# A feed-forward layer by seven block products, with the second's right sides kept in DRAM

## The chip, the core and the metric

The kernel runs on one core of one Trainium2 chip. The metric is the device time of one execution in microseconds (us). Three runs of the kernel before took 1964.12, 1957.71 and 1943.81 us, median 1957.71.

## What is computed

One layer of a hybrid decoder over x of 1024 positions by 1024 features in float32, D_FF = 2816. The change touches only the last lines:

```
x = x + merged @ w_out[l]
h = rms_norm(x, norm2_g[l])
z = h @ w_ffn_in[l]
x = x + (jax.nn.silu(z[..., :D_FF]) * z[..., D_FF:]) @ w_ffn_out[l]
...
return rms_norm(x, final_g)
```

Ahead of them stand a state-space branch, dilated attention and a convolution branch, whose outputs are merged; the change leaves these as they are.

## The kernel before

Everything lies transposed: 128 features on the partitions, positions along the columns. Activations are eight tiles of 128 x 1024, handled in two halves of 512 columns. Each float32 matmul is made of three on a faster format: a number is split into a high part (a copy rounded to that format) and a low part (the number less the high part), and TensorE sums high x high, high x low and low x high. One weight tile holds up to four 128 x 128 blocks (256 KB): `weights` loads it on SyncE's queue, ScalarE copies the high part (L95), GpSimd subtracts for the low part (L96); two buffers for the load, three each for the parts. `gemms` then issues three matmuls for each block and half (L125 to L127).

`out_proj` adds the product with w_out to x and keeps x1 on the chip (tiles xa); `norm2` scales it (L861, on VectorE, with the factor in PSUM) and splits it into fh and fl (L862 ScalarE, L863 VectorE and GpSimd in turn). `ffn` goes over the 22 units of 128 of D_FF in three groups of 7, 7 and 8 (FFG). `act(j)` makes the two products of a unit, 96 matmuls, and from them silu(a) x b: a tanh on ScalarE (L894), two VectorE operations that read PSUM (L895, L896), and the split into gh (L897) and gl (L898). After each group the second product of that group is added to x1 for all eight m (L938). In the last group the second half of m = 4 to 7 is made in two quarters of 256 columns from weights kept split (`weights_kept`), and `final_norm` (L940) of the first half and of a quarter runs beside matmuls; that of the last quarter ends the kernel. `rstd` (from L130) makes the norm's factor: small matmuls with ones (L139), some small VectorE operations and one ScalarE root, and small matmuls that spread the factor (L154).

Each engine works through its instructions in the order of its own list, which a scheduler makes from the program; a tile's next use waits for its last reader.

## Time and profile before

| | |
|---|---|
| median of three runs | 1957.71 us |
| the profiled execution | 1964.32 us, span 1962.2 us |
| instructions | 23791 |
| busy: PE, VectorE, ScalarE, GpSimd | 96%, 47%, 28%, 31% of the span |
| DMA | 128.97 MB, mean 66 GB/s |
| most of the chain that ended last | PE 72%, of it the three matmul lines L125 to L127 65% |

PE is TensorE's matmul side, PEld its weight loads, DVE VectorE, ACT ScalarE, POOL GpSimd, SP SyncE. A row of the trace gives an operation's line, engine, output and inputs, its size and how long it took. Matmuls are pipelined: one that takes 0.39 us may start 0.23 us after the one before.

### The profile page before, as it was taken

The page shows a single profiled execution, that of the slowest core. Times are in us where ns is not written, and L with a number is a line of the kernel's source. Part 1 is how long each engine was busy: PE and PEld are TensorE (multiplying, and loading weights), DVE is VectorE, ACT ScalarE, POOL GpSimd, SP SyncE. Part 2 cuts the span into 40 slices and gives each one's busy share as a digit, 9 for nine tenths or more (in the row PEclk, how much of TensorE's full clock was granted, in tenths as well). Part 3 has the DMA queues.
Part 4 walks back from the last instruction along what each step waited for, and adds up shares of the span by engine and source line. Part 5 has one row for each costly group of instructions (what it writes and reads, how often), then busy time and mean ns, then how long its engine had stood idle before and what let it go on. Part 6 is the DMA issues. An engine that isn't in the chain of part 4 may idle for free.

```text
span 1962.2 us, 23791 instructions
## 1 busy us (share of the span) xinstructions
PE 1884.1 (96%) x8956; PEld 1492.1 (76%) x8956; DVE 924.3 (47%) x1913; ACT 541.4 (28%) x1023; POOL 601.5 (31%) x519
## 2 busy tenths in 40 slices
...
PEclk9899999897999999899899999999999999999999
...
GB/s 158 97 124 33 39 54 33 70 22 22 28 108 86 54 49 79 57 58 58 81 49 48 49 140 123 87 54 48 48 51 49 49 45 47 54 48 49 49 97 134
DMA packets 94898, 128.97 MB, mean 66 GB/s; under 512 B 14264, under 2 KB 44088, under 8 KB 94784
## 3 DMA queue, kind: packets, MB, share of 16 engines
...
q8 instruction: 71, 1.16, 0.2%
...
## 4 chain that ended last, share of the span: by engine, by line
PE 72%; DVE 7%; POOL 1%; DMA 1%; ACT 1%; issue 1%; SPq 0%; DVEq 0%; ACTq 0%; POOLq 0%
PE ps L126 22%; PE ps L127 22%; PE ps L125 21%; PE ps L388 1%; PE ps L339 1%; DVE zw L644 1%; DVE es L763 1%; POOL wlo L96 1%; PE ps L403 1%; PE ps L768 1%; DVE z L751 1%; PE ps L391 1%; DMA t<-in_xt 1%; PE ps L369 0%; POOL fl L863 0%
## 5 line engine op out<-in xcount | busy, mean ns | idle before, releaser
L96 POOL TENSOR_TENSOR wlo<-wraw,whi 128x512 fp32r<-128x512 f32 x336 | 453.9, 1352 | 1065.8 <-ACT whi L95 1055.0
L95 ACT ACTIVATE whi<-wraw 128x512 fp32r<-128x512 f32 x334 | 208.5, 625 | 828.8 <-PE ps L126 629.5
L125 PE MATMUL ps<-hh,whi 128*128 128x512 f32 x832 | 334.5, 402 | 11.1 <-ACT whi L95 6.3
L126 PE MATMUL ps<-hl,whi 128*128 128x512 f32 x832 | 335.1, 403 | 5.3 <-DVE hl L251 5.3
L127 PE MATMUL ps<-hh,wlo 128*128 128x512 f32 x832 | 332.7, 400 | 0.0
L126 PE MATMUL ps<-fl,whi 128*128 128x512 f32 x704 | 274.1, 389 | 0.5 <-POOL fl L863 0.5
L127 PE MATMUL ps<-fh,wlo 128*128 128x512 f32 x704 | 274.1, 389 | 0.1
L125 PE MATMUL ps<-fh,whi 128*128 128x512 f32 x704 | 274.0, 389 | 0.0
L125 PEld LDWEIGHTS ps<-hh,whi 128*128 128x128 f32 x832 | 159.7, 192 | 50.4 <-issue 9.6
L126 PEld LDWEIGHTS ps<-hl,whi 128*128 128x128 f32 x832 | 159.7, 192 | 42.1 <-DVE hl L251 7.3
L127 PEld LDWEIGHTS ps<-hh,wlo 128*128 128x128 f32 x832 | 159.7, 192 | 37.3 <-issue 5.8
L479 DVE SCALAR_TENSOR_TENSOR cy<-cx,hcw,cy 128x1024 f32<-128x1024 f32 x120 | 165.8, 1382 | 1.0
L126 PEld LDWEIGHTS ps<-fl,whi 128*128 128x128 f32 x704 | 132.2, 188 | 28.3 <-POOL fl L863 0.9
L127 PEld LDWEIGHTS ps<-fh,wlo 128*128 128x128 f32 x704 | 132.2, 188 | 28.3 <-POOL wlo L96 0.9
L125 PEld LDWEIGHTS ps<-fh,whi 128*128 128x128 f32 x704 | 132.2, 188 | 27.3
L125 PE MATMUL ps<-gh,whi 128*128 128x512 f32 x320 | 124.6, 389 | 0.0
L126 PE MATMUL ps<-gl,whi 128*128 128x512 f32 x320 | 124.6, 389 | 0.0
L127 PE MATMUL ps<-gh,wlo 128*128 128x512 f32 x320 | 124.5, 389 | 0.0
L895 DVE SCALAR_TENSOR_TENSOR t<-t,ps 128x512 f32<-128x512 f32 x44 | 30.2, 687 | 187.6 <-ACT t L894 187.6
L938 DVE SCALAR_TENSOR_TENSOR xa<-ps,xa 128x512 f32<-128x512 f32 (+1 forms) x52 | 33.8, 650 | 165.0 <-PE ps L127 165.0
L125 PE MATMUL ps<-ah,whi 128*128 128x512 f32 x256 | 102.1, 399 | 2.6 <-ACT ah L820 2.6
L126 PE MATMUL ps<-al,whi 128*128 128x512 f32 x256 | 102.0, 398 | 1.1 <-DVE al L821 1.1
...
## 6 DMA issues: line engine op xcount, KB each, us to landing
wraw<-in_win SPq DMA_DIRECT2D x120, 256.0 KB, 2.8
wraw<-in_wffi SPq DMA_DIRECT2D x96, 256.0 KB, 2.8
wraw<-in_wffo SPq DMA_DIRECT2D x40, 256.0 KB, 2.6
wraw<-in_wout SPq DMA_DIRECT2D x32, 256.0 KB, 2.8
wraw<-in_wglu SPq DMA_DIRECT2D x16, 256.0 KB, 2.6
t<-in_xt SPq DMA_DIRECT2D x16, 256.0 KB, 3.2
x<-in_xt SPq DMA_DIRECT2D x7, 512.0 KB, 6.8
...
```

The costliest lines, as they stand in the source:

```text
L95: eng.tensor_copy(h, r) if eng else self.A.activation(h, r, AF.Copy)
L96: self.G.tensor_tensor(out=l, in0=r, in1=h.bitcast(F32), op=ALU.subtract)
L125: self.PE.matmul(o, hi[:, k, :], xh[k0 + k][:, t], start=first, stop=False)
L126: self.PE.matmul(o, hi[:, k, :], xl[k0 + k][:, t], start=False, stop=False)
L127: self.mm = self.PE.matmul(o, lo[:, k, :], xh[k0 + k][:, t], start=False, stop=last).ins
L339: self.PE.transpose(ps[:, a, k, :], pt[:, a, k * P:(k + 1) * P], self.ident)
L388: PE.matmul(s[:, 0:256], q1[r, r4, par].rearrange("p b i -> p (b i)"), kp[r, 2 * r4:2 * r4 + 2, :], start=True, stop=True)
L391: PE.matmul(s[c, 256:320], q2[r, r4, par, b], kp[r, j, b::2], start=True, stop=True)
L403: PE.matmul(pv[64 * a:64 * a + 64, (j % 4) * P:(j % 4 + 1) * P], vp[:, 2 * r4 + k, 64 * a:64 * a + 64], ptt[:, a, k, :], start=k == 0, sto ...
L479: V.scalar_tensor_tensor(out=cy, in0=cx[:, j:j + T], scalar=self.hcw[:, ct * TAPS + j:ct * TAPS + j + 1], in1=cy, op0=ALU.mult, op1=ALU.add)
L895: V.scalar_tensor_tensor(out=w, in0=w, scalar=1.0, in1=a, op0=ALU.add, op1=ALU.mult)
L938: self.V.scalar_tensor_tensor(out=x, in0=ps, scalar=0.5, in1=x, op0=ALU.mult, op1=ALU.add)
```

## The change

Both products of the feed-forward layer are made by Strassen's scheme in Winograd's form: the weights are seen as 2 x 2 blocks b11, b12, b21, b22, the right side as well, and seven products of sums of blocks take the place of eight products. The products run in the order 1, 5, 2, 6, 4, 3, 7 and add up in four banks of PSUM (u, y, v, z), which are read between products. For the first product a unit's block rows are its two weight rows j and 22 + j, the block columns of the right side are the two halves of the positions, and the inner blocks are features 0 to 511 and 512 to 1023. A unit now has seven split left sides of 128 x 512 where it had four, three of which are plain weights and four sums (`total`, on VectorE, tile wsum).

The right sides: `norm2(1)` turns x1 in place into the sums and splits them into f1 to f7 (`put`), so x1 is written to DRAM before (xd) and read back later. For the second product `sides(p)` makes seven right sides from units p and p + 11 (tiles ct), each a high and a low part (g1 to g7, 512 KB), writes them to DRAM (ad) and `load_sides` reads them back for groups of pairs (0, 1, 2), (3, 4, 5), (6, 7, 8), (9, 10); pairs 0 and 2 stay on the chip. 17 + 20 slots of 512 KB (l, r) hold all of this; during the first product two of the l slots are free for the seven sides of a pair. `ffn_out` makes two m at a time, 63 matmuls over three pairs or 42 over two; parts of its results go through ScalarE and GpSimd (`aside`). The first products 1 and 2 of three units run before the second half's norm is there (AHEAD). m = 4 to 7 of the last group are made in the old way, in pieces of 512, 256 and 256 columns (`tail`). Weights have six load buffers and four for each part; the pools of the branches are closed before out_proj and new ones opened. `rstd` has two small operations less. The diff's core:

```diff
-FFG = (7, 7, 8)
+NPR = NFF // 2
+GROUPS = ((0, 1, 2), (3, 4, 5), (6, 7, 8), (9, 10))
+AHEAD = 3
...
+KEPT = (0, 2)
+PRODUCTS = (1, 5, 2, 6, 4, 3, 7)
+BANK = {1: "u", 6: "u", 7: "u", 5: "y", 3: "y", 2: "v", 4: "z"}
...
+        def total(p, a, b, op):
+            left[p] = self.wtile("wsum", n)
+            V.tensor_tensor(out=left[p], in0=a, in1=b, op=op)
+            return left[p]
+        for p in sums:
+            if p in (1, 2, 4):
+                left[p] = load({1: 11, 2: 12, 4: 22}[p])
+            elif p == 5:
+                total(5, load(21), load(22), ALU.add)
+            elif p == 6:
+                total(6, left[5], load(11), ALU.subtract)
+                total(7, load(11), load(21), ALU.subtract)
+            elif p == 3:
+                total(3, load(12), left[6], ALU.subtract)
+            hi, lo = self.wtile("whi", n, F32R), self.wtile("wlo", n, F32R)
+            self.split(left[p], hi, lo, self.G)
+            b = BANK[p]
+            first = b not in banks
+            if first:
+                banks[b] = self.psum()
+            o = banks[b]
+            for k, (xh, xl) in enumerate(xc[p]):
+                PE.matmul(o, hi[:, k, :], xh, start=first and k == 0, stop=False, skip_group_check=not first)
+                PE.matmul(o, hi[:, k, :], xl, start=False, stop=False, skip_group_check=not first)
+            for k, (xh, xl) in enumerate(xc[p]):
+                self.mm = PE.matmul(o, lo[:, k, :], xh, start=False, stop=k == n - 1, skip_group_check=not first).ins
+            after[p](banks)
...
+    def right_sides(self, b11, b12, b21, b22, put):
+        V = self.V
+        put(1, b11)
+        V.tensor_tensor(out=b11, in0=b12, in1=b11, op=ALU.subtract)
+        put(5, b11)
+        put(2, b21)
+        V.tensor_tensor(out=b11, in0=b22, in1=b11, op=ALU.subtract)
+        put(6, b11)
+        V.tensor_tensor(out=b21, in0=b21, in1=b11, op=ALU.subtract)
+        put(4, b21)
+        put(3, b22)
+        V.tensor_tensor(out=b12, in0=b22, in1=b12, op=ALU.subtract)
+        put(7, b12)
...
+            early.close()
+            self.bufs = {"wraw": 6, "wsum": 3, "whi": 4, "wlo": 4, "t2": 6, "ct": 6, "g": 6, "s": 2, "l": 17, "r": 20}
+            self.wp = enter(pool("w2"))
+            self.pp = enter(tc.tile_pool(name="ps2", bufs=1, space=PSUM, reuse_waits="tile"))
+            self.lp2 = enter(pool("left"))
+            self.out_proj()
+            right.close()
+            self.rp2 = enter(pool("right", "right"))
+            self.ffn()
+            self.fill(self.rp2, 32)
...
+        def put(p, src, side, eng):
+            z = self.slot(side, f"f{p}")
+            self.split(src, z[:, 0], z[:, 1], eng)
+            self.h2.setdefault(p, []).append((z[:, 0], z[:, 1]))
+        if h == 0:
+            for k in range(KD):
+                scale(k)
+                put(1 if k < half else 2, x1[k][:, 0], "l", self.G if k % 2 else V)
+            return
+        b = [[x1[k][:, 0], x1[k][:, 1], x1[k + half][:, 0], x1[k + half][:, 1]] for k in range(half)]
+        for k, (b11, b12, b21, b22) in enumerate(b):
+            scale(k)
+            V.tensor_tensor(out=b11, in0=b12, in1=b11, op=ALU.subtract)
+            put(5, b11, "r", self.G)
+            scale(k + half)
+            V.tensor_tensor(out=b11, in0=b22, in1=b11, op=ALU.subtract)
+            put(6, b11, "r", self.G)
+        for b11, b12, b21, b22 in b:
+            V.tensor_tensor(out=b21, in0=b21, in1=b11, op=ALU.subtract)
+            put(4, b21, "r", V)
+        for k, (b11, b12, b21, b22) in enumerate(b):
+            put(3, b22, "r", self.G if k % 2 else V)
+        for k, (b11, b12, b21, b22) in enumerate(b):
+            V.tensor_tensor(out=b12, in0=b22, in1=b12, op=ALU.subtract)
+            put(7, b12, "r", self.G if k % 2 else V)
...
+        def silu(x):
+            w = self.tmp([P, 512])
+            A.activation(w, x, AF.Tanh, scale=0.5)
+            V.scalar_tensor_tensor(out=x, in0=w, scalar=1.0, in1=x, op0=ALU.add, op1=ALU.mult)
+        def add(key, b, then=None):
+            def f(banks):
+                V.tensor_tensor(out=r[key], in0=banks[b], in1=r[key], op=ALU.add)
+                if then:
+                    then(r[key])
+            return f
+        def end(banks):
+            for x, key in (("m", "z"), ("n", "y")):
+                add(key, "u")(banks)
+                o = self.wp.tile([P, 512], F32, tag="ct", name="ct", bufs=self.bufs["ct"])
+                V.scalar_tensor_tensor(out=o, in0=r[key], scalar=0.5, in1=r[x], op0=ALU.mult, op1=ALU.mult)
+                self.act.setdefault(j, []).append(o)
+        after = {1: copy("m", "u"), 5: copy("y", "y"), 2: add("m", "v", silu), 6: copy("n", "u"), 4: copy("z", "z"),
+                 3: add("n", "y", silu), 7: end}
+        return self.wino(blocks, half, self.h2, after, banks, skip, only), r
...
+    def sides(self, p):
+        def put(q, src):
+            z = self.slot("r" if p == KEPT[1] and q > 1 else "l", f"g{q}")
+            self.split(src, z[:, 0], z[:, 1], self.V)
+            if p in KEPT:
+                self.first[p, q] = z
+            else:
+                self.nc.sync.dma_start(out=self.ad[p, q], in_=z.bitcast(F32))
+        (b11, b12), (b21, b22) = self.act.pop(p), self.act.pop(p + NPR)
+        if p in GROUPS[-1]:
+            put(0, b12)
+        self.right_sides(b11, b12, b21, b22, put)
+    def load_sides(self, group, products):
+        xc = {}
+        for q in products:
+            for p in group:
+                if p in KEPT:
+                    z = self.first[p, q]
+                else:
+                    z = self.slot("l" if p % 4 == 0 or (p % 4 == 3 and q == 1) else "r", f"g{q}")
+                    self.nc.sync.dma_start(out=z.bitcast(F32), in_=self.ad[p, q])
+                xc.setdefault(q, []).append((z[:, 0], z[:, 1]))
+        return xc
...
+        self.act, self.first = {}, {}
+        order = [j for p in (KEPT[0], *(p for p in range(NPR) if p not in KEPT), KEPT[1]) for j in (p, p + NPR)]
+        begun = {}
+        for j in order[:AHEAD]:
+            begun[j] = self.ffn_in(j, only=(1, 2))
+            if j == order[0]:
+                self.norm2(1)
+        for n, j in enumerate(order):
+            banks, kept = begun.get(j, (None, None))
+            self.ffn_in(j, banks, skip=(1, 2) if banks else (), kept=kept)
+            if n % 2:
+                self.sides(j - NPR)
+        self.x1 = [self.slot("l", "xa", F32) for _ in range(KD)]
+        self.ss = self.slot("l", "ss", F32)
+        for group in GROUPS:
+            last = group is GROUPS[-1]
+            xc = self.load_sides(group, PRODUCTS)
+            n, p0 = len(group), group[0]
+            for m in range(0, KD - KEEP if last else KD, 2):
+                if p0 == 0:
+                    for mm in (m, m + 1):
+                        self.nc.sync.dma_start(out=self.x1[mm], in_=self.xd[mm])
+                self.ffn_out(m, p0, n, xc)
+                if last:
+                    for mm in (m, m + 1):
+                        for h in range(2):
+                            self.sumsq(mm, h)
+        self.tail(p0, n, xc, self.load_sides(group, (0,))[0])
...
+        def aside(x, b):
+            c = self.tmp([P, 512])
+            A.activation(c, b, AF.Copy)
+            G.tensor_tensor(out=x, in0=x, in1=c, op=ALU.add)
+        def end(banks):
+            add(x21, banks["u"])
+            aside(x22, banks["u"])
+        after = {1: lambda b: add(x11, b["u"]), 5: lambda b: aside(x22, b["y"]), 2: lambda b: add(x11, b["v"]), 6: lambda b: add(x12, b["u"]),
+                 4: lambda b: add(x21, b["z"]), 3: lambda b: add(x12, b["y"]), 7: end}
+        self.wino(blocks, n, xc, after)
...
+        for h, t in ((0, slice(0, 512)), (1, slice(0, 256)), (1, slice(256, 512))):
+            for m, (hi, lo) in enumerate(kept, KD - KEEP):
+                ps = self.psum()[:, 0:t.stop - t.start]
+                for k, (xh, xl) in enumerate(halves[h]):
+                    self.PE.matmul(ps, hi[:, k, :], xh[:, t], start=k == 0, stop=False)
+                    self.PE.matmul(ps, hi[:, k, :], xl[:, t], start=False, stop=False)
+                    self.mm = self.PE.matmul(ps, lo[:, k, :], xh[:, t], start=False, stop=k == 2 * n - 1).ins
+                x = self.x1[m][:, h, t]
+                V.tensor_tensor(out=x, in0=ps, in1=x, op=ALU.add)
+                self.sumsq(m, h, t)
+                if m == KD - KEEP and (h, t.start) != (0, 0):
+                    self.final_norm(0 if t.start == 0 else 1, slice(0, 512) if t.start == 0 else slice(0, 256), self.mm)
+        self.final_norm(1, slice(256, 512))
```

Three places in VectorE's list. The first is where the second half's right sides are made. Before (t2 is the scaled tile, L861 scales, L863 splits; then the first unit's silu):

```order
L861 SCALAR_TENSOR_TENSOR t2_9896<-xa3_9005,vecs_66,ps_9879 128x512
L863 TENSOR_TENSOR fl2_9021<-t2_9892,fh2_9013 128x512
L861 SCALAR_TENSOR_TENSOR t2_9900<-xa4_9006,vecs_66,ps_9879 128x512
L861 SCALAR_TENSOR_TENSOR t2_9904<-xa5_9007,vecs_66,ps_9879 128x512
L861 SCALAR_TENSOR_TENSOR t2_9908<-xa6_9008,vecs_66,ps_9879 128x512
L863 TENSOR_TENSOR fl4_9023<-t2_9900,fh4_9015 128x512
L861 SCALAR_TENSOR_TENSOR t2_9912<-xa7_9009,vecs_66,ps_9879 128x512
L863 TENSOR_TENSOR fl6_9025<-t2_9908,fh6_9017 128x512
L895 SCALAR_TENSOR_TENSOR t2_9990<-t2_9990,ps_9916 128x512
L896 TENSOR_TENSOR t2_9990<-t2_9990,ps_9953 128x512
L898 TENSOR_TENSOR gl_9776<-t2_9990,gh_9769 128x512
```

After (the end of the same work: f4, f3, f7 are low parts, L965 the last sums of blocks; the scales and the sums of L954 to L960 stand ahead of these rows; m_9914 is a result of the second unit, wsum_10053 the weight sum of the first unit's third product):

```order
L109 TENSOR_TENSOR f4_9852<-xa_9009,f4_9852 128x512
L109 TENSOR_TENSOR f4_9856<-xa_9010,f4_9856 128x512
L109 TENSOR_TENSOR f4_9860<-xa_9011,f4_9860 128x512
L109 TENSOR_TENSOR f4_9864<-xa_9012,f4_9864 128x512
L109 TENSOR_TENSOR f3_9867<-xa_9009,f3_9867 128x512
L109 TENSOR_TENSOR f3_9873<-xa_9011,f3_9873 128x512
L965 TENSOR_TENSOR xa_9007<-xa_9011,xa_9007 128x512
L109 TENSOR_TENSOR f7_9880<-xa_9005,f7_9880 128x512
L965 TENSOR_TENSOR xa_9008<-xa_9012,xa_9008 128x512
L109 TENSOR_TENSOR f7_9888<-xa_9007,f7_9888 128x512
L1003 TENSOR_TENSOR m_9914<-ps_9922,m_9914 128x512
L128 TENSOR_TENSOR wsum_10053<-wraw_10051,wsum_10010 128x512
```

The first unit's next weight sum has moved behind all of the right sides.

The second place is a unit in the middle of the first product. Before, three operations follow each other for each half of a unit: the two of silu and the low part.

```order
L895 SCALAR_TENSOR_TENSOR t2_9990<-t2_9990,ps_9916 128x512
L896 TENSOR_TENSOR t2_9990<-t2_9990,ps_9953 128x512
L898 TENSOR_TENSOR gl_9776<-t2_9990,gh_9769 128x512
L895 SCALAR_TENSOR_TENSOR t2_10070<-t2_10070,ps_9996 128x512
L896 TENSOR_TENSOR t2_10070<-t2_10070,ps_10033 128x512
```

After (one stretch of a unit that follows a pair's end: ct are the unit's results, g the low parts of the right sides, L163 to L168 their sums, wsum the next unit's weight sums, m a result read from PSUM):

```order
L1012 SCALAR_TENSOR_TENSOR ct_10839<-z_10798,m_10709 128x512
L1012 SCALAR_TENSOR_TENSOR ct_10842<-y_10734,n_10779 128x512
L128 TENSOR_TENSOR wsum_11055<-wraw_11051,wraw_11053 128x512
L109 TENSOR_TENSOR g2_10853<-ct_10839,g2_10853 128x512
L163 TENSOR_TENSOR ct_10685<-ct_10842,ct_10685 128x512
L168 TENSOR_TENSOR ct_10688<-ct_10842,ct_10688 128x512
L165 TENSOR_TENSOR ct_10839<-ct_10839,ct_10685 128x512
L109 TENSOR_TENSOR g6_10858<-ct_10685,g6_10858 128x512
L128 TENSOR_TENSOR wsum_11099<-wsum_11055,wraw_11030 128x512
L1003 TENSOR_TENSOR m_10895<-ps_10928,m_10895 128x512
L109 TENSOR_TENSOR g4_10863<-ct_10839,g4_10863 128x512
L128 TENSOR_TENSOR wsum_11101<-wraw_11030,wraw_11051 128x512
```

The work on the sides stands between the weight sums and the reads of PSUM that the next products need.

The third place is the change from the first to the second product (the last pair's sides; ps_13628 is bank u, which product 6 of the second product adds to next):

```order
L1012 SCALAR_TENSOR_TENSOR ct_13567<-z_13526,m_13437 128x512
L1012 SCALAR_TENSOR_TENSOR ct_13570<-y_13462,n_13507 128x512
L128 TENSOR_TENSOR wsum_13768<-wraw_13764,wraw_13766 128x384
L109 TENSOR_TENSOR g2_13579<-ct_13567,g2_13579 128x512
L163 TENSOR_TENSOR ct_13413<-ct_13570,ct_13413 128x512
L168 TENSOR_TENSOR ct_13416<-ct_13570,ct_13416 128x512
L165 TENSOR_TENSOR ct_13567<-ct_13567,ct_13413 128x512
L109 TENSOR_TENSOR g6_13583<-ct_13413,g6_13583 128x512
L109 TENSOR_TENSOR g4_13587<-ct_13567,g4_13587 128x512
L109 TENSOR_TENSOR g3_13590<-ct_13570,g3_13590 128x512
L109 TENSOR_TENSOR g7_13594<-ct_13416,g7_13594 128x512
L1083 TENSOR_TENSOR xa_13597<-ps_13628,xa_13597 128x512
```

The first read of bank u (L1083) stands behind the last pair's low parts g2, g6, g4, g3 and g7; before, there was no such place, since a group's low parts came one at a time.

## Rows read from the trace of the kernel before

**Rows 1.** The page: busy time and share of each engine; granted clock in tenths.

```profile
PE 1884.1 (96%) x8956; PEld 1492.1 (76%) x8956; DVE 924.3 (47%) x1913; ACT 541.4 (28%) x1023; POOL 601.5 (31%) x519
PEclk9899999897999999899899999999999999999999
```

**Rows 2.** Stretches: length, busy time and count of PE, PEld, DVE, ACT, POOL; clock, DMA share, GB/s.

```profile
8.00:12.00 4.00, 3.83 (x12) 2.66 (x13) 2.24 (x4) 2.97 (x4) 2.51 (x2) 1.00 1.03 412
...
1222.00:1262.00 40.00, 37.88 (x175) 30.52 (x174) 20.13 (x30) 20.01 (x31) 23.77 (x17) 1.00 0.29 97
1262.00:1900.00 638.00, 638.00 (x2816) 528.47 (x2815) 125.69 (x169) 134.22 (x222) 165.35 (x132) 1.00 0.17 53
...
1927.10:1951.40 24.30, 24.30 (x205) 24.29 (x204) 14.99 (x36) 7.49 (x16) 0.00 (x0) 1.00 0.22 71
1951.40:1962.20 10.80, 1.85 (x14) 1.52 (x13) 4.62 (x15) 0.62 (x2) 0.00 (x0) 0.70 0.29 97
```

**Rows 3.** Grouped lines from 1222 us on: count, busy us, mean ns, idle before.

```profile
L96 POOL TENSOR_TENSOR wlo<-wraw,whi 128x512 fp32r<-128x512 f32 x135 | 176.2, 1306 | 432.4 <-ACT whi L95 426.9 <-DMA wraw<-in_wffi 2.8 <-PE ps L126 2.7
...
L95 ACT ACTIVATE whi<-wraw 128x512 fp32r<-128x512 f32 x134 | 84.6, 632 | 338.6 <-PE ps L126 239.4 <-issue 79.3 <-DMA wraw<-in_wffi 16.6
...
L898 DVE TENSOR_TENSOR gl<-t,gh 128x512 fp32r<-128x512 f32 x44 | 39.3, 892 | 34.7 <-ACT gh L897 34.7
...
L896 DVE TENSOR_TENSOR t<-t,ps 128x512 f32<-128x512 f32 x44 | 30.2, 687 | 149.1 <-PE ps L127 148.8
...
L894 ACT ACTIVATE t<-ps 128x512 f32<-128x512 f32 x44 | 26.0, 591 | 47.8 <-PE ps L127 45.8 <-POOL fl L863 1.9
...
L96 POOL TENSOR_TENSOR wlo<-wraw,whi 128x384 fp32r<-128x384 f32 x16 | 16.2, 1012 | 64.6 <-ACT whi L95 64.6
...
L947 DVE SCALAR_TENSOR_TENSOR o<-xa,vecs,ps 128x256 f32<-128x256 f32 x16 | 6.4, 475 | 2.1 <-PE ps L154 2.1
...
L861 DVE SCALAR_TENSOR_TENSOR t<-xa,vecs,ps 128x512 f32<-128x512 f32 x8 | 5.6, 739 | 1.3 <-PE ps L154 1.3
...
L938 DVE SCALAR_TENSOR_TENSOR xa<-ps,xa 128x256 f32<-128x256 f32 x8 | 3.4, 422 | 6.1 <-PE ps L127 6.1
```

**Rows 4.** Timeline of DVE and POOL: start, duration (us), engine, line, operation.

```profile
1244.78 1.12 DVE L863 TENSOR_TENSOR fl<-t,fh 128x512 fp32r<-128x512 f32 x1
1245.31 1.75 POOL L96 TENSOR_TENSOR wlo<-wraw,whi 128x512 fp32r<-128x512 f32 x1
...
1263.83 1.30 POOL L96 TENSOR_TENSOR wlo<-wraw,whi 128x512 fp32r<-128x512 f32 x1 [1.79 <-ACT whi L95]
1264.30 1.37 DVE L898 TENSOR_TENSOR gl<-t,gh 128x512 fp32r<-128x512 f32 x1 [2.76 <-ACT gh L897]
...
1283.15 1.30 POOL L96 TENSOR_TENSOR wlo<-wraw,whi 128x512 fp32r<-128x512 f32 x1 [4.15 <-ACT whi L95]
1283.59 0.69 DVE L895 SCALAR_TENSOR_TENSOR t<-t,ps 128x512 f32<-128x512 f32 x1 [2.31 <-ACT t L894]
...
1292.16 0.69 DVE L898 TENSOR_TENSOR gl<-t,gh 128x512 fp32r<-128x512 f32 x1 [0.70 <-ACT gh L897]
```

**Rows 5.** Timeline, second half's norm2: its first scale and its last split.

```profile
1241.54 2.06 DVE L861 SCALAR_TENSOR_TENSOR t<-xa,vecs,ps 128x512 f32<-128x512 f32 x3 [1.31 <-PE ps L154]
...
1249.98 1.73 POOL L863 TENSOR_TENSOR fl<-t,fh 128x512 fp32r<-128x512 f32 x1
```

**Rows 6.** DMA issues: count, KB of one, median us from issue to landing.

```profile
wraw<-in_wffi SPq DMA_DIRECT2D x96, 256.0 KB, 2.8
...
x<-in_xt SPq DMA_DIRECT2D x7, 512.0 KB, 6.8
...
ud<-uw SPq DMA_DIRECT2D x4, 512.0 KB, 3.0
```

**Rows 7.** Timeline, the end: first add after the last matmul, last norm's scales.

```profile
1951.66 0.42 DVE L938 SCALAR_TENSOR_TENSOR xa<-ps,xa 128x256 f32<-128x256 f32 x1 [1.45 <-PE ps L127]
...
1955.71 3.22 DVE L947 SCALAR_TENSOR_TENSOR o<-xa,vecs,ps 128x256 f32<-128x256 f32 x8 [0.87 <-PE ps L154]
```

212 lines of the change are left out of this document (97 added, 115 removed).

## The prediction

> **What bounds the kernel now.** I read the busy times and the clock first: TensorE is busy 96% of the span, at close to the full granted clock [rows 1]. The feed-forward part is then cut into stretches [rows 2]. It begins at 1222.0. From 1262 to 1900 TensorE is never idle: 2816 matmuls in 638.0 us, one every 0.2266 us, at the full 2.4 GHz (granted clock 1.00). VectorE is busy 20% there, ScalarE 21%, GpSimd 26%, and DMA moves 53 GB/s. In the 24.3 us from 1927.1 to 1951.4 it makes 205, of which 192 are over 256 columns and the rest small ones of the norm: 0.12 us each. After the last one, 10.8 us of closing norm and output follow [rows 2, 7]. So this part is bound by the count of matmuls, and each one less gives its 0.2266 us for as long as the other engines hand over operands in time.
>
> **What is removed.** Before, each of 22 units takes 96 matmuls in the first product and 48 in the second: 3072 of 512 columns and 192 of 256. After: 22 x 84 = 1848 in the first; 4 x 63 x 3 + 2 x 42 = 840 in the second's seven-product part; in the tail 48 of 512 and 96 of 256 columns. That is 336 full and 96 half matmuls less: 336 x 0.2266 + 96 x 0.120 = 76.1 + 11.5 = 87.6 us. This is the most the change can give.
>
> **What is added, in the steady state of the first product.** A unit now lasts 84 x 0.2266 = 19.0 us, a pair 38.1. In a pair ScalarE makes 14 weight copies, 12 moves out of PSUM or tanh and 7 side copies, some 20 us by [rows 3] (0.63 and about 0.6 each): half of the time. GpSimd subtracts 14 weights x 1.30 = 18.2 us. VectorE does 8 additions that read PSUM (0.69) and 27 operations whose two inputs both lie in SBUF: 8 weight sums, 8 of the gate, 4 sums and 7 low parts of the right sides.
>
> The second kind has no fixed price. In [rows 4] one took 0.69 us with GpSimd idle. The one at 1264.30 came while GpSimd subtracted (1263.83 to 1265.13) and ended at 1265.67, 0.54 us after it: it had waited. At 1244.78 and 1245.31 it goes the other way too: GpSimd's 1.75 us end 1.16 us after VectorE's end. A PSUM reader inside such a time (1283.59) keeps its 0.69. So the two engines take turns, at about 0.54 and 1.16 us. A pair needs 27 x 0.54 + 14 x 1.16 = 30.8 us of turns out of 38.1: 81%, which fits. VectorE's own time is 27 x 0.89 (the mean with GpSimd at 26%) + 8 x 0.69 = 29.6 us at the low end; with 1.0 each 32.5; at the 1.37 of a full wait 42.5, over the pair's 38.1. I take 1.0: GpSimd is about half busy, and half of the 0.68 lies between 0.69 and 1.37. PE then loses only small waits. I put them at 5 us over the eleven pairs, with 0 and 49 us (11 x 4.4) as ends.
>
> The Trainium skill (GPSIMD Engine Reference, Key points) says that GpSimd shares its SBUF interfaces with VectorE and contends with VectorE instructions that have two SBUF inputs. The trace agrees (0.69 against 1.37 us). That rule speaks against this change; what it could cost is the first rival below.
>
> **The sides' way through DRAM.** Only two slots take each pair's seven 512 KB tiles, so the third must wait for the first's write. By order and durations, with 0 at a unit's last matmul: the third side's low part ends at 4.9, is in DRAM at 7.9 (3.0 us [rows 6]), the fifth's copy can start then, and ScalarE reaches it at 8.8; it waits about 1 us for the sixth and hardly for the seventh. Behind these copies on ScalarE stand weight copies that PE wants 5 to 10 us later (four buffers of 2.7 us). A stall begins where a write takes about 8 us. Rate: 65 writes and their reads are 34 MB each; a pair moves 8 weight tiles and 7 sides, 5.7 MB in 38 us, 150 GB/s, against 412 GB/s in the opening burst [rows 2]. I cost it at nothing, with rival 2 as the other end.
>
> **The second product.** A pair of rows m lasts 63 x 0.2266 = 14.3 us. GpSimd: 7 x 1.01 + 2 x 1.3 to 1.5 = 10 us. VectorE: 6 x 0.69 + 4 x about 0.6 = 6.6. Both fit. At a group's change 21 sides are wanted; seven load ahead, the other 14 (7.3 MB, 18 us at 412 GB/s) while the last 14.3 us of the old group free their slots, in the order of use. The last is wanted 12 us into the new group: no wait. If they started only there, 18 - 12 = 6 us at each of three changes: ends 0 and 18 us, an end of the range and no case of its own.
>
> **Where PE must wait anew.**
> 1. norm2 of the second half. In the kernel before eight scales and eight splits there took from 1241.5 to 1251.7 [rows 5], and PE lost 2.1 us in the stretch [rows 2]. Now the third product's weight sum of the first unit stands on VectorE behind all work on the right sides (first order piece): 8 scales x 0.74, 24 operations with two SBUF inputs, which alternate with GpSimd's 12 splits and 3 weights (24 x 0.54 + 15 x 1.16 = 30 us of turns). Adding the steps gives the sum at about 31 us after the scale factor is there, its high and low part at 33 to 34, and the seventh product's end at 37. PE has 87 matmuls = 19.7 us of work for that time. Wait: 17 us (12 if all run at 0.69 and 1.30; 20 at most). I add 3 us for a lower granted clock after it (it was 0.70 in the closing stretch, where PE was mostly idle), ends 0 and 7, and 3 for the small matmuls of the norm, which exist before too.
> 2. From the first to the second product. TensorE (PE in the rows) has 18 matmuls (4.1 us) and then the second side's 9 (2 us). The add that frees bank u for product 6 stands behind nine operations with two SBUF inputs (third piece): 2 x 0.69 + 11 x 0.7 = 9.3 us without, about 12.5 with waits for GpSimd. Wait: 12.5 - 6.1 = 6 us (3 to 8).
> 3. At out_proj the new pools start on freed memory, so the third weight load waits for the branches' end: one load and split, 2.5 us (0 to 6).
> 4. The tail. PE needs 96 x 0.120 = 11.5 us for the half matmuls, but VectorE has the whole first half's final norm now beside them (8 x 0.74 = 5.9), the next quarter's (8 x 0.475 = 3.8), eight adds and six sums at 0.42 (5.9) and two chains of small ones (2): 17.6 us, then the closing 10.8. With 1 to 2 us of waits that is 30 us, 8 more than PE's count gives.
>
> **The sum.** 1222.0 + 2.5 + 2736 full matmuls x 0.2266 (620.0) + norm2 17 + 3 + 3 + transition 6 + small waits 5 + tail 30 = 1908.5 us of span. Before: 1962.2, with 2.1 us around it (time 1964.3). So 1910.6 against 1964.3: 53.7 us less. The profiled execution is as slow as the slowest of the three runs (1964.1); set against the median of 1957.7 the same gain ends at 1904. I say 1906.
>
> **The rivals.**
> 1. GpSimd and VectorE block each other: VectorE's operations with two SBUF inputs take over 1.21 us in the mean ((38.1 - 5.5) / 27), and VectorE sets the pace. At 1.25 to 1.37, +12 to +49 us: 1918 to 1955. For: single rows at 1.37. Against: 81% of turns, and L898's mean of 0.89 [rows 3]. 18%.
> 2. Slower: the two write-back slots. If a 512 KB write beside weight loads takes more than 8 us, ScalarE stands in its order before the copy of the fifth side and the weights behind it come late. At 11 us the four rounds cost about 6 us in each of nine to ten pairs, +57: 1963 and more. For: a 512 KB load took 6.8 us in the burst. Against: the writes in the trace took 3.0, at a third of the burst's rate. 8%.
> 3. The new waits are mostly hidden (norm2 at 8, transition 2, tail 3 less): about 1888. 12%.
>
> **How the numbers follow.** The forecast has 60% (1893 to 1920); 2% are for what I don't see. Leaving out rival 2 and the dearer half of rival 1 gives the range 1880 to 1945. A measurement can tell about 1% here, that is 20 us. Faster by more (under 1938): forecast, rival 3 and nearly half of rival 1, 80%. Within 1%: most of the rest of rival 1, 11%. Slower: rival 2 and a little of rival 1, 9%.
>
> **What would show it.** 84 matmuls in 19.0 us with no gap in the middle of the first product (right), or PE gaps released by GpSimd's wlo or VectorE's wsum (rival 1). wlo near 1.5 and the side subtractions near 1.0 us. Writes of the sides at 3 us to landing, ScalarE's waits for them under 2 us a pair (else rival 2). A gap of some 17 us, in pieces, at the right sides of norm2, 6 us at the change of product, none at the group changes. VectorE busy to the end of the tail. I am wrong above all if VectorE and GpSimd queue on each other more than one operation deep.

## The result, and the profile after

The changed kernel takes 1904.0 us in the median (runs of 1930.33, 1897.12, 1907.48 and 1900.52). The kernel before, measured beside it, takes 1957.8 us. The ratio is 0.972, with a 95% interval from 0.965 to 0.980. The ratio leaves out the run of 1930.33 us, which was in the slow state. So the change makes the kernel 2.8% faster, and the forecast of 1906 us holds.

The profile shown here is that of the 1930.33 us execution. Between 500 and 600 us its granted clock was 0.81, in work that the change does not touch, so all that follows starts late. Therefore I compare lengths of stages between events and not the times at which they happen. The page first: busy times, the granted clock in tenths, then the issues of the new transfers (count, KB of one, median us from issue to landing).

```profile
PE 1824.1 (95%) x8524; PEld 1430.1 (74%) x8524; DVE 1214.8 (63%) x2271; ACT 668.6 (35%) x1282; POOL 776.9 (40%) x659
...
PEclk9899999897969999999999999979999999999998
...
ad<-g SPq DMA_DIRECT2D x65, 512.0 KB, 2.8
g<-ad SPq DMA_DIRECT2D x65, 512.0 KB, 6.7
```

Against [rows 1], TensorE (PE) has 432 matmuls fewer and is busy 60 us less. VectorE (DVE) is busy 290 us more and GpSimd (POOL) 175 us more. The feed-forward part runs from its first matmul at 1241.2 to the end at 1928.5: 687.3 us, where it took 740.2 before (1222.0 to 1962.2). That is 52.9 us less. It falls into a first product of 445.1 us (to the first matmul that reads a side g), a second of 200.0 (to the first of the tail) and a tail of 42.2.

The stretches of that part, as in [rows 2]: length, busy time and count of PE, PEld, DVE, ACT and POOL, then granted clock, DMA share and GB/s.

```profile
1256.00:1300.00 44.00, 28.52 (x95) 19.60 (x94) 37.79 (x42) 20.41 (x35) 27.26 (x20) 0.77 0.10 33
1300.00:1685.00 385.00, 384.56 (x1697) 318.19 (x1697) 288.16 (x362) 187.90 (x338) 201.11 (x143) 1.00 0.43 154
1685.00:1700.00 15.00, 10.18 (x38) 7.97 (x37) 10.34 (x16) 5.81 (x11) 4.18 (x4) 0.89 0.89 331
...
1886.10:1911.80 25.70, 25.70 (x174) 23.74 (x172) 18.28 (x35) 9.02 (x18) 1.30 (x1) 1.00 0.19 68
1911.80:1928.50 16.70, 4.26 (x23) 3.85 (x21) 9.27 (x30) 0.97 (x4) 0.00 (x0) 0.59 0.43 147
```

In the second row lies nearly the whole first product: 385 us in which PE is idle for 0.44 us, with a matmul every 0.227 us at the full clock, while VectorE is busy 75% of the time. So the saving of the removed matmuls arrives whole in the steady state. What is given back lies at three places: the norm of the second half (first row), the change from the first product to the second (third row), and the tail (the last two). Of the 87.6 us that the removed matmuls are worth, this part gives back 34.7: by the stages about 20 at the norm (22.5 less the 2.1 lost there before), 6 at the change of product and 9 in the tail.

PE's four longest waits from 1200 us on (engine, line, what it waited for: total us, times, longest) name them:

```profile
PE ps L149 <- DVE m L1003: 9.0, 1, 9.0
PE ps L214 <- DVE sm L208: 5.1, 2, 3.2
PE ps L149 <- DMA g<-ad: 4.8, 1, 4.8
PE ps L150 <- POOL f L109: 4.2, 5, 1.5
```

The first and the fourth are the norm, the third is the change of product, the second is the closing norms.

### The profile page after: what moved, and what is told of

Its sections match the earlier page's. It is cut to its first block, busy times and chain, and to the rows that moved or that the text cites. A ratio compares the mean times of both kernels' runs of the same rounds, so it can differ in the third digit from the quotient of the medians.

```text
span 1928.5 us, 24417 instructions
## 1 busy us (share of the span) xinstructions
PE 1824.1 (95%) x8524; PEld 1430.1 (74%) x8524; DVE 1214.8 (63%) x2271; ACT 668.6 (35%) x1282; POOL 776.9 (40%) x659
## 4 chain that ended last, share of the span: by engine, by line
PE 45%; DVE 2%; issue 1%; DMA 1%; POOL 1%; ACT 0%; SPq 0%; DVEq 0%; ACTq 0%; POOLq 0%
PE ps L149 10%; PE ps L150 10%; PE ps L152 10%; PE ps L188 4%; PE ps L187 4%; PE ps L186 4%; DVE f L109 0%; PE ps L1115 0%; PE ps L1116 0%; PE ps L1117 0%; DMA g<-ad 0%; POOL f L109 0%; DVE o L1133 0%; PE ps L200 0%; PE ps L214 0%
## 5 line engine op out<-in xcount | busy, mean ns | idle before, releaser
L103 POOL TENSOR_TENSOR wlo<-wraw,whi 128x512 fp32r<-128x512 f32 x184 | 257.8, 1404 | 574.8 <-ACT whi L102 569.2
L186 PE MATMUL ps<-hh,whi 128*128 128x512 f32 x832 | 334.9, 403 | 11.2 <-ACT whi L102 6.3
L102 ACT ACTIVATE whi<-wraw 128x512 fp32r<-128x512 f32 x182 | 114.0, 629 | 418.7 <-PE ps L187 335.6
L149 PE MATMUL ps<-f,whi 128*128 128x512 f32 x616 | 242.4, 394 | 11.7 <-DVE m L1003 9.0
L150 PE MATMUL ps<-f,whi 128*128 128x512 f32 x616 | 242.3, 393 | 4.2 <-POOL f L109 4.2
L109 POOL TENSOR_TENSOR wlo<-wsum,whi 128x512 fp32r<-128x512 f32 (+2 forms) x144 | 179.3, 1250 | 158.2 <-ACT whi L108 104.3
L186 PEld LDWEIGHTS ps<-hh,whi 128*128 128x128 f32 x832 | 160.0, 192 | 50.7 <-issue 10.3
L109 POOL TENSOR_TENSOR wlo<-wraw,whi 128x512 fp32r<-128x512 f32 (+2 forms) x108 | 142.2, 1317 | 99.4 <-ACT whi L108 66.7
L152 PE MATMUL ps<-f,wlo 128*128 128x512 f32 x616 | 165.8, 391 | 0.0
L149 PEld LDWEIGHTS ps<-f,whi 128*128 128x128 f32 x616 | 116.7, 189 | 38.0 <-ACT f L108 13.0
L150 PEld LDWEIGHTS ps<-f,whi 128*128 128x128 f32 x616 | 116.6, 189 | 31.3 <-POOL f L109 7.5
L152 PEld LDWEIGHTS ps<-f,wlo 128*128 128x128 f32 x616 | 116.2, 189 | 24.1
L149 PE MATMUL ps<-g,whi 128*128 128x512 f32 x280 | 109.9, 393 | 4.9 <-DMA g<-ad 4.8
L108 ACT ACTIVATE whi<-wsum 128x512 fp32r<-128x512 f32 (+2 forms) x144 | 82.9, 578 | 84.0 <-PE ps L150 69.4
L150 PE MATMUL ps<-g,whi 128*128 128x512 f32 x280 | 109.4, 391 | 0.0
```

The lines of the kernel that those rows point to most:

```text
L102: eng.tensor_copy(hi, raw) if eng else self.A.activation(hi, raw, AF.Copy)
L103: self.G.tensor_tensor(out=lo, in0=raw, in1=hi.bitcast(F32), op=ALU.subtract)
L108: self.A.activation(hi, src, AF.Copy)
L109: eng.tensor_tensor(out=lo, in0=src, in1=hi.bitcast(F32), op=ALU.subtract)
L149: PE.matmul(o, hi[:, k, :], xh, start=first and k == 0, stop=False, skip_group_check=not first)
L150: PE.matmul(o, hi[:, k, :], xl, start=False, stop=False, skip_group_check=not first)
```

## Experiments

All of them start from the changed kernel. Where only one profile was taken, a whole time tells little, since the granted clock between 200 and 600 us differs from run to run (0.91 to 1.00) and moves the start of the feed-forward part (1209.7 to 1241.2 us in these profiles). Inside that part the stages repeat where an edit leaves them alone: the first product within about 0.5 us, the tail within 0.7 and the second product within 1.6 (199.4 to 201.0). The verdicts rest on them. Three kernels with four times each come last.

| kernel | time, us | first product | second product | tail |
|---|---|---|---|---|
| the changed kernel, profiled | 1930.33 | 445.1 | 200.0 | 42.2 |
| e1_bank | 1901.09 | 445.3 | 200.1 | 41.9 |
| e2_wsum_pool | 1930.23 | 457.5 | 204.2 | 42.1 |
| e5_hook | 1898.87 | 444.5 | 201.0 | 42.0 |
| e6_f56_vector | 1914.36 | 443.6 | 200.3 | 41.9 |
| e7_write2 | 1903.95 | 445.7 | 201.0 | 41.9 |
| e3_write3 | 1980.65 | 511.8 | 203.7 | 41.8 |
| e8_loads_outproj | 1899.44 | 445.5 | 195.5 | 42.3 |
| e4_tail_halves | 1902.84 | 445.2 | 199.4 | 44.3 |
| e9_ahead4 | 1921.80 | 447.7 | 200.8 | 42.1 |
| e10_three | 1908.68 (median) | 448.7 | 195.8 | 42.3 |
| e11_five | 1905.75 (median) | 441.7 | 196.0 | 42.3 |
| e12_four | 1897.70 (median) | 442.7 | 197.1 | 42.5 |

### Who ends the wait at norm2

The longest wait, 9.0 us, ends with an add that reads a PSUM bank (m, L1003). The prediction had named another operation, the weight sum of product 3. Both stand on VectorE behind the work on the right sides. The first run writes `norm2(1)` one unit later in the program, so that the second unit's add comes ahead of the sides.

```diff
...
             if j == order[0]:
-                self.norm2(1)
+                bc = self.rstd(self.squares.pop(0), D, self.mm)
+            if j == order[1]:
+                self.norm2(1, bc)
```

> In the changed kernel PE waits 9.0 us at product 4 of the first unit, and the trace names the VectorE addition of m (L1003) as what ended it: the second unit's product 2 still holds the PSUM bank that product 4 wants, and its reader stands on VectorE behind all of the right sides' work. Here the norm's factor is made at the same place, but the work on the right sides is written behind the second unit's first two products, so that this one read moves ahead of it; nothing else changes. Theory A (the bank): the 9.0 us split: product 4 starts when its fourth side is split, some 5 us earlier, and PE then waits 4 to 6 us for the third product's weight sum, which is still last; the stretch from the factor to the seventh product's end (about 39 us) is 1 to 3 us shorter. Theory B (the weight sum alone decides, as the prediction had it): the end of the seventh product does not move (within 0.7 us), though product 4 may move. Rival C (the order matters for neither, the turns of VectorE and GpSimd do): no wait changes by more than 1 us.

The wait for m is gone, and another stands 12 matmuls later, at product 3 of the same unit:

```profile
PE ps L149 <- ACT whi L108: 6.0, 1, 6.0
```

This is the high part of product 3's weight sum. The first product takes 445.3 us, as before. So the bank was merely the first of two operations in one queue, and taking it away shortens nothing.

The second run moves all weight sums from VectorE to GpSimd.

```diff
-            V.tensor_tensor(out=left[p], in0=a, in1=b, op=op)
+            self.G.tensor_tensor(out=left[p], in0=a, in1=b, op=op)
```

> All weight sums (4 a unit) are made by GpSimd and no longer by VectorE. If the two engines take turns at 0.54 us (VectorE) and 1.16 us (GpSimd) for operations with two SBUF inputs, a pair's turns grow from 27 x 0.54 + 14 x 1.16 = 30.8 us to 19 x 0.54 + 22 x 1.16 = 35.8 us of the pair's 38.1, 94%, and GpSimd's own time is 22 x 1.3 to 1.4 = 29 to 31 us. Theory A (turns): it still just fits; PE loses 0 to 1.5 us in a pair, 0 to 15 us over the first product (385 us between 1300 and 1685 in the changed kernel), and wlo's mean rises towards 1.4. Theory B (engines independent, only own time counts): no loss at all, VectorE at 50% and wlo at 1.30. Theory C (a chain of three GpSimd steps for a product is too late whatever the shares): over 2 us a pair, over 22 us in all. In the second product GpSimd gets 11 x about 1.0 + 2 x 1.5 = 14 us for 14.3 us of matmuls, so PE waits there too, 0 to 2 us a pair of rows, 14 pairs.

The first product grows by 12.4 us and the second by 4.2. GpSimd's sides come late (PE waits 8.7 us for POOL f, 4.2 before), the wait for m stays at 8.3, and waits for low parts and loads grow. In the middle of the product GpSimd is now busy 335 of 385 us (201 before), and the same operations take longer on both engines (grouped lines of this run between 1283 and 1668 us: count, busy us, mean ns, idle before):

```profile
L109 DVE TENSOR_TENSOR g<-ct,g 128x512 fp32r<-128x512 f32 x73 | 95.5, 1311 | 44.4 <-ACT g L108 44.2
L109 POOL TENSOR_TENSOR wlo<-wsum,whi 128x512 fp32r<-128x512 f32 x81 | 129.4, 1598 | 34.7 <-ACT whi L108 33.9 <-PE ps L152 0.5
```

In the changed kernel these means are 875 and 1375 ns. So the theory of independent engines is refuted, and the loss lies in the range of the theory of turns. Work that goes from one of the two engines to the other does not leave the turns that both take. How much of the 12.4 us is waiting for turns the run does not tell, since GpSimd also needs about 1.3 us for an operation that VectorE makes in 0.69.

The third run writes product 3's weight sum and the adds ahead of the last eight sides (f3 and f7), so that both known waits are served early.

```diff
...
+            if p in hooks:
+                hooks[p]()
...
```

The hook makes f3 and f7, behind the split of product 3's weight sum.

> Only the order around the first unit's third product is changed: the fourth sides are split first, then the weight sum of product 3 and its split, and only then the third and seventh sides; the second and third unit's additions of m, which free PSUM banks, come ahead of these too. The run before this one freed the bank alone, and PE's 9.0 us at product 4 turned into 6.0 us at product 3, with the first product's length unchanged (445.4 against 445.1 us). Theory (the place in VectorE's order decides, as the prediction said, with two things behind the sides' work, a bank and a weight sum): now both are ahead, product 4 starts some 5 us earlier, product 3 follows within 1 to 3 us, and the first product (first to last of its matmuls) takes 437 to 440 us, 5 to 8 us less. Rival (the amount of work on VectorE and GpSimd in turns is what lasts, wherever the sum stands): the seventh sides come last in any order, less than 2 us gained.

Both waits are gone, and the first product is only 0.6 us shorter, hardly more than it repeats within. The whole first product, in the changed kernel and in this run (columns as above):

```profile
1241.20:1686.34 445.14, 429.22 (x1873) 351.54 (x1872) 334.28 (x418) 216.95 (x386) 234.32 (x166) 0.98 0.40 142
```

```profile
1209.69:1654.17 444.48, 433.32 (x1874) 352.34 (x1872) 321.03 (x418) 220.22 (x386) 242.09 (x166) 0.98 0.40 142
```

PE's idle time did fall, from 15.9 to 11.2 us, but its matmuls take 4.1 us more. The stretch from 1226.5 to 1268.5 holds 97 matmuls in 42 us at a granted clock of 0.76, much as the 44 us of the changed kernel hold 95 at 0.77, although it has 9.5 us of idle time and not 15.5. The idle time is in more pieces, and the last matmul before each piece counts with its whole length (0.39 us at the full clock and not 0.227). The rows don't divide these two. VectorE's rows show where the pieces come from (start, duration, engine, line, operation, what it waited for):

```profile
1236.55 0.69 DVE L959 TENSOR_TENSOR xa<-xa 128x512 f32<-128x512 f32 x1 [1.36 <-POOL f L109]
...
1249.41 1.18 DVE L970 TENSOR_TENSOR xa<-xa 128x512 f32<-128x512 f32 x1
1250.51 1.76 DVE L109 TENSOR_TENSOR f<-xa,f 128x512 fp32r<-128x512 f32 x1
```

Operations of one shape take 0.69, 1.18 or 1.76 us, by what GpSimd does beside them. The wait has been cut into pieces that the next operations of the same queue end. The fourth run takes work out of the turns instead: the eight low parts of sides 5 and 6 are made on VectorE, at 0.69 us each, and no longer on GpSimd at 1.3.

```diff
-            put(5, b11, "r", self.G)
+            put(5, b11, "r", V)
...
-            put(6, b11, "r", self.G)
+            put(6, b11, "r", V)
```

> In the second half's norm2 the low parts of the fifth and sixth sides (8 operations) are made by VectorE and no longer by GpSimd. If the engines take turns at 0.54 and 1.16 us, the turns fall from 24 x 0.54 + 15 x 1.16 = 30.4 to 32 x 0.54 + 7 x 1.16 = 25.4 us, while VectorE's own list grows from 24 x 0.69 + 8 x 0.74 = 22.5 to 28 us without waits. Theory A (turns): VectorE waited for GpSimd most of the difference before, so the stretch stays within 2 us of what it was (first product 445 us, 443 to 446), though GpSimd does 8 operations less. Theory B (independent engines, VectorE's own time decides): 5.5 us longer, 450 to 451. Theory C (GpSimd's part was the bound, its low part of each side had to be there before the next sum in place): 4 us or more shorter, under 441.

The first product is 1.5 us shorter, within the range of the theory of turns (443 to 446) and against that of independent engines (450 to 451). Here too PE's idle time falls by more, from 15.9 to 12.0 us, and its matmuls take 2.4 us longer; in the first of the four runs the two are 13.0 and 3.1. Together: no single operation sets the length of the norm. Three edits took 2.9 to 4.8 us of idle time away, slower matmuls took most or all of it back, and the gain is 1.5 us or nothing. That the rest is set by the amount of work in turns fits these rows but is not shown: the third run ends its last side 4.5 us later than the changed kernel (50.7 us after the first matmul, against 46.2) and loses nothing by it.

### The two slots and the writes to DRAM

The prediction's rival on the slow side put a threshold at a write of 8 us. Two runs write each side again into other DRAM tiles, which makes the time longer for which a slot is held, and adds DMA traffic and issues on SP.

```diff
...
                 self.nc.sync.dma_start(out=self.ad[p, q], in_=z.bitcast(F32))
+                self.nc.sync.dma_start(out=self.ad2[p, q], in_=z.bitcast(F32))
+                self.nc.sync.dma_start(out=self.ad3[p, q], in_=z.bitcast(F32))
```

The last line stands in the run with three writes alone. Two writes:

> Each right side is written to DRAM twice. With one write (2.8 us to landing) PE lost nothing in the middle of the first product, with three (a slot held 5.3 to 7.1 us from the first issue to the last landing) it lost 66.8 us, so the point at which the two slots decide lies below 7 us and not at the 8 us of the prediction. Here a slot is held about 4 to 4.5 us. If the loss begins in proportion from about 3 us on: 20 to 30 us lost (first product 465 to 475 us). If there is a point near 5 us, below which the weight loads behind the writes on SyncE's queue still come in time: 0 to 8 us lost (445 to 453).

The first product takes 445.7 us. A write lands in 4.2 us in the median, and a slot is held, from the first issue to the last landing, for 5.0 us in the median (4.0 to 7.4). ScalarE's waits for the writes grow only from 11.8 to 13.3 us in all. Three writes:

> Each split right side is written to DRAM three times (to three places) where the changed kernel writes it once, so a slot comes free only when all three writes have landed; DMA in the first product rises from about 154 to about 350 GB/s. This puts the two write-back slots to the test. Theory A (the slack worked out before: no stall until a write takes about 8 us): the three land 5 to 8 us after the first is issued, ScalarE's waits for them grow from 12 us in all to 40 to 80 us, and PE loses 0 to 10 us in the first product. Rival (slots are the next bound, little slack): PE loses over 2 us a pair, 20 us and more. The weights' loads, from 2.8 us to landing, may rise to 4 to 5 us; they have six buffers.

Now the first product takes 66.7 us more: 53.6 of idle PE and 13.1 of slower matmuls. Most of the idle time is one kind of wait (total us, times, longest), and the chain that ends the longest one shows how it comes about (start, us, what):

```profile
PE ps L149 <- ACT whi L108: 53.4, 7, 25.2
```

```profile
1634.16 4.43 DMA ad<-g
...
1638.69 0.64 ACT g L108
1639.35 0.70 DVE g L109
1640.07 0.32 SPq L1029
...
1641.43 4.91 DMA ad<-g
...
1650.83 4.93 DMA wraw<-in_wffi
...
1655.85 0.70 DVE wsum L128
...
1656.64 0.64 ACT whi L108
1657.32 0.79 PE ps L149
```

A write frees its slot, ScalarE and VectorE make the next side in it, and SP issues that side's writes. The next weight load stands behind them on SP, and PE waits for its sum. The mechanism of the rival is right, but its threshold was too high: slots held for 5.0 us in the median cost nothing, and slots held for 6.8 us in the median (5.2 to 8.9) cost 66.7 us. The two ranges overlap, and both are wider than the expectations have them (4 to 4.5 and 5.3 to 7.1 us), so no single time is shown to be the limit. The three writes also fill the DMA (0.73 busy against 0.43, and weight loads land in 4.2 us instead of 2.8), so a part of that price may be the loads'. These runs don't divide it.

### The change of product, and out_proj

At the change of product PE waited 4.82 us for a load of a side (DMA g<-ad), and not for the add on VectorE that the prediction had named. The loads of pair 1 were issued together from 1685.40 on, behind a weight load on SP. At out_proj, PE waited for the high part of a weight:

```profile
1143.85 0.39 PE L188 MATMUL ps<-ah,wlo 128*128 128x512 f32 x1
1148.76 0.79 PE L186 MATMUL ps<-mh,whi 128*128 128x512 f32 x1 [4.52 <-ACT whi L102]
1149.35 0.63 PE L187 MATMUL ps<-ml,whi 128*128 128x512 f32 x1
```

That weight copy stands on ScalarE behind a copy of mh that is ready only at 1147.56. One run removes both causes: it loads pair 1's sides ahead of the last pair's sides, and makes the high part of out_proj's first two weights on GpSimd.

```diff
+            if p == KEPT[1] and q == 5:
+                for i in PRODUCTS:
+                    self.first[1, i] = self.slot("r", f"g{i}")
+                    self.nc.sync.dma_start(out=self.first[1, i].bitcast(F32), in_=self.ad[1, i])
...
-                hi, lo = self.ahead.pop(0) if self.ahead else self.weights(src[:, k0:k0 + m, :], m)
+                hi, lo = self.ahead.pop(0) if self.ahead else self.weights(src[:, k0:k0 + m, :], m, self.engs.pop(0) if self.engs else None)
...
+        self.engs = [self.G, self.G]
...
-                if p in KEPT:
+                if (p, q) in self.first:
```

> Two edits in places far apart. First, the seven loads of pair 1's sides for the first group of the second product are put ahead of the last pair's own sides, so that they take slots that come free 13.6 us before the change of product and stand ahead of weight loads on SyncE's queue. In the changed kernel PE waits 4.8 us there for such a load, issued at 1685.4, when PE was already through with the first product. Theory (the loads stood behind a weight load that waited for its buffer): the wait for a load goes, and what remains is the read of bank u behind the last sides on VectorE, 2 to 4 us, as the prediction had it at 6: 1 to 3 us gained. Rival (DMA has no room there, 331 GB/s in that stretch): the loads land as late as before. Second, the first two weights of out_proj get their high part on GpSimd and not on ScalarE. In the changed kernel PE waits 4.5 us there: ScalarE's copy stands behind the last high part of the merged activations. Theory (order on ScalarE): the wait shrinks to under 1 us and the half clock after it goes, 4 to 6 us gained. Rival (the buffers, closed pools): the wait stays above 3 us.

The second product is 4.5 us shorter, more than the theory's 1 to 3. The wait for the loads is gone, and a smaller one is left there, for a side that VectorE makes last:

```profile
PE ps L151 <- DVE g L110: 1.9, 1, 1.9
```

At out_proj the 4.5 us are gone as well, and the way from the first mh matmul to the feed-forward part takes 91.0 us instead of 92.4 (91.1 in the kernel before). Thus out_proj cost 4.5 + 1.4 = 5.9 us, the second part as matmuls at the lower of the two clock levels after the gap (0.43 us apart instead of 0.227). The gain at out_proj holds with the six raw-weight buffers of this run; with five, below, more than half of it is lost.

### The tail

The tail makes its last 512 columns in two pieces of 256. This run makes them whole.

```diff
-        for h, t in ((0, slice(0, 512)), (1, slice(0, 256)), (1, slice(256, 512))):
+        for h, t in ((0, slice(0, 512)), (1, slice(0, 512))):
...
```

> The tail's last 512 columns are made whole instead of in two quarters (48 matmuls of 512 columns for 96 of 256), so one final norm of 512 columns closes the kernel where two of 256 did. In the changed kernel the stretch from 1886.1 to the end takes 42.4 us: 25.7 with PE busy, then 16.7, in which VectorE still has the quarter before last. Theory A (VectorE is the tail's bound, PE's count is not): VectorE saves one chain of small operations and 16 x 0.475 become 8 x 0.74, three adds and sums fall away; the closing stretch shrinks to 12 to 14 us and the PE stretch to 22 to 23, 35 to 37 in all: 5 to 7 us gained. Theory B (the quarters hide half of the last norm, as in the kernel before): 4 to 6 us lost, since a whole norm of 512 columns (5.9 us) stands behind the last matmul instead of 3.2.

The tail grows by 2.1 us: the way of theory B, though less than its 4 to 6, and against theory A. The rows of VectorE show it (start, duration, engine, line, operation):

```profile
1877.52 5.36 DVE L1133 SCALAR_TENSOR_TENSOR o<-xa,vecs,ps 128x512 f32<-128x512 f32 x8 [0.33 <-PE ps L214]
1882.80 1.28 DVE L1119 TENSOR_TENSOR xa<-ps,xa 128x512 f32<-128x512 f32 x2
...
1891.62 5.36 DVE L1133 SCALAR_TENSOR_TENSOR o<-xa,vecs,ps 128x512 f32<-128x512 f32 x8 [2.23 <-PE ps L214]
```

The first half's closing norm, 5.36 us, stands ahead of the last adds in both kernels. In whole columns the second one takes 5.36 us at the very end, where the pieces leave 3.22.

### One more unit ahead, and the edits together

The products 1 and 2 of three units run ahead of the sides. A fourth needs one more buffer for t2, which comes from the raw weights.

```diff
-AHEAD = 3
+AHEAD = 4
...
-            self.bufs = {"wraw": 6, "wsum": 3, "whi": 4, "wlo": 4, "t2": 6, "ct": 6, "g": 6, "s": 2, "l": 17, "r": 20}
+            self.bufs = {"wraw": 5, "wsum": 3, "whi": 4, "wlo": 4, "t2": 7, "ct": 6, "g": 6, "s": 2, "l": 17, "r": 20}
```

> One more unit's products 1 and 2 are multiplied ahead of the norm (AHEAD 4 instead of 3; one raw-weight slot less and one more t2 slot for it): 24 more matmuls of 0.226 us, 5.4 us, move into the time in which VectorE and GpSimd make the seven sides, and 24 fewer stand behind it. Theory A (PE waits there because the work of VectorE and GpSimd between the scale factor and the last sides takes longer than the products that are ahead; nothing else waits): the first product takes 440 (445.1 minus 5.4). Theory B (the unit's 24 weights need sums and splits by the same engines that make the sides, so the cover brings its own work with it): each of its products 1 and 2 needs weight sums on VectorE and low parts on GpSimd, and the first product stays within 1.5 us of 445.

Neither theory is right: the first product takes 447.7, which is 2.6 us more. PE's order tells why nothing is gained. Only product 1 of the fourth unit stands ahead; its product 2 stands behind product 6 of the first unit, and PE waits there for a bank:

```profile
1277.61 0.80 PE L149 MATMUL ps<-f,whi 128*128 128x512 f32 x1 [7.29 <-DVE m L1003]
```

```profile
1286.75 0.77 PE L149 MATMUL ps<-f,whi 128*128 128x512 f32 x1 [9.02 <-DVE m L1003]
```

The first row is of this run, the second of the changed kernel. In both, PE has made 96 matmuls of the first product by then. That took 48.2 us here (from 1229.38) and 45.6 there (from 1241.20). The cover didn't grow: the fourth unit's 12 matmuls took the place of 12 others (product 5 of the first unit), and the bank came 2.7 us later. Whether the unit's own weights or the raw-weight buffer that it cost made the bank late is not shown, as the run changes both.

Three edits together (the fourth unit, the earlier loads, out_proj's weights):

> Three edits together: one more unit ahead of the norm, pair 1's sides loaded ahead of the last sides' writes, and the high part of the first two out_proj weights on GpSimd. Theory A (the three waits are apart and their gains add): transition -4.5, out_proj's wait -4.5 to -5.5, the norm between 0 and -5.4: 1889 to 1895 beside a run of the changed kernel at 1900.5, ratio to before about 0.966. Theory B (taking one wait away only moves it to the next): 1897 or more.

The ratio to the kernel before is 0.973 (0.969 to 0.978), not to be told from the changed kernel's. The expectation was put in whole times, and its case for 1897 or more came true. By stages the first two edits do about what they did alone: 448.7 in the first product (e9: 447.7) and 195.8 in the second (e8: 195.5). At out_proj they do not. PE waits there again, for the high part that GpSimd now makes, and the way from the first mh matmul to the feed-forward part takes 94.7 us (e8: 91.0):

```profile
1134.80 0.80 PE L187 MATMUL ps<-mh,whi 128*128 128x512 f32 x1 [2.68 <-POOL whi L103]
```

With five raw-weight buffers the second weight's load is issued 5.3 us later than in e8, just when the first mh matmul starts. So the buffer that the fourth unit took brings back more than half of what the edit at out_proj gained. From the end of the matmuls before out_proj to the end of the kernel the three edits save 2.8 us, which the whole times can't show.

Five edits (those three, the weight sum ahead of f3 and f7, and sides 5 and 6 on VectorE):

> The three edits of the run before, and the two that gave 0.6 and 1.5 us in the first product (product 3's weight sum written ahead of the last sides; the low parts of products 5's and 6's sides on VectorE). Theory A (all add): 1887 to 1893, 2 us under the three. Theory B (the order at the norm is used up, as the amount of work in turns sets its end): within 1.5 us of the three edits' time.

The ratio is 0.973 (0.968 to 0.979), and the median 2.9 us below that of the three. By stages the first product falls by 7.0 us against the three edits, to 441.7, which is more than the 2.1 that the two added edits gave alone. Neither theory had that. Out_proj still takes 94.8 us.

Four edits (the five without the fourth unit):

> The five edits without the fourth unit ahead of the norm. With it the run of one edit lost 2.6 us in the first product (447.7 against 445.1) and the run of five gained 3.4 (441.7). Theory A (the fourth unit ahead holds two more PSUM banks until the sides are done, so that it only moves the wait, and it loses the same 2.6 us among the five): without it the first product takes 439. Theory B (once product 3's weight sum and the sides' low parts are out of the turns, the banks come free in time and the fourth unit's 24 matmuls do cover something): without it the first product takes 443.0, that is 445.1 minus the 0.6 and 1.5 that the two edits gave alone. Second product 195.5 and tail 42.3 by both.

The first product takes 442.7, as the theory of added gains has it (445.1 - 0.6 - 1.5 = 443.0). So in the first product the fourth unit costs 2.6 us alone and gains 1.0 beside the other four edits. The ratio is 0.971 (0.964 to 0.978). By stages this version's feed-forward part takes 682.3 us and that with five edits 679.9, against 687.3. But with six raw-weight buffers out_proj takes 91.0 us again, against 94.8 with five, and from the first mh matmul to the end the four edits need 773.3 us and the five 774.7: with the buffer that it costs, the fourth unit gains nothing. The whole times can't tell these from the changed kernel: the start of the feed-forward part spreads over more than they gain.

## Why the prediction was right

**The steady state.** The prediction took VectorE's operations with two SBUF inputs at 1.0 us in the mean, GpSimd's subtractions near 1.5, and small waits of 5 us. The grouped lines between 1300 and 1685 us (count, busy us, mean ns, idle before):

```profile
L109 DVE TENSOR_TENSOR g<-ct,g 128x512 fp32r<-128x512 f32 x74 | 64.4, 875 | 22.4 <-ACT g L108 22.0
L128 DVE TENSOR_TENSOR wsum<-wsum,wraw 128x512 f32<-128x512 f32 x20 | 29.9, 1495 | 21.5 <-POOL wlo L109 21.5
L1012 DVE SCALAR_TENSOR_TENSOR ct<-y,n 128x512 f32<-128x512 f32 x21 | 29.7, 1416 | 0.0
L128 DVE TENSOR_TENSOR wsum<-wraw 128x512 f32<-128x512 f32 x39 | 28.6, 735 | 1.8 <-POOL wlo L109 1.8
L128 DVE TENSOR_TENSOR wsum<-wraw,wsum 128x512 f32<-128x512 f32 x20 | 26.9, 1345 | 25.6 <-POOL wlo L109 25.6
L1012 DVE SCALAR_TENSOR_TENSOR ct<-z,m 128x512 f32<-128x512 f32 x21 | 15.2, 723 | 0.0
L999 DVE SCALAR_TENSOR_TENSOR n<-t,n 128x512 f32<-128x512 f32 x21 | 14.5, 692 | 14.1 <-ACT t L998 14.0
L1003 DVE TENSOR_TENSOR z<-ps,z 128x512 f32<-128x512 f32 x21 | 14.4, 685 | 2.5 <-PE ps L152 2.5
...
L999 DVE SCALAR_TENSOR_TENSOR m<-t,m 128x512 f32<-128x512 f32 x19 | 13.0, 684 | 0.7
...
L160 DVE TENSOR_TENSOR ct<-ct 128x512 f32<-128x512 f32 x11 | 7.6, 692 | 0.4
L168 DVE TENSOR_TENSOR ct<-ct 128x512 f32<-128x512 f32 x10 | 6.8, 678 | 0.0
L163 DVE TENSOR_TENSOR ct<-ct 128x512 f32<-128x512 f32 x10 | 6.8, 678 | 0.0
L165 DVE TENSOR_TENSOR ct<-ct 128x512 f32<-128x512 f32 x10 | 6.8, 677 | 0.0
```

```profile
L109 POOL TENSOR_TENSOR wlo<-wsum,whi 128x512 fp32r<-128x512 f32 x82 | 112.1, 1375 | 114.1 <-ACT whi L108 89.4 <-PE ps L152 15.7 <-PE ps L150 9.0
L109 POOL TENSOR_TENSOR wlo<-wraw,whi 128x512 fp32r<-128x512 f32 x58 | 89.1, 1537 | 64.9 <-ACT whi L108 43.8 <-PE ps L152 14.7 <-DVE ct L165 3.6
```

The mean of a form depends on where it stands: 0.74 us for a weight sum whose turn comes while GpSimd is idle, 1.50 for one that mostly meets a subtraction. The twelve VectorE rows without ps, all that have two SBUF inputs of 512 columns, have a mean of 250.2 / 276 = 0.91 us, and the two of GpSimd 201.2 / 140 = 1.44. The 1.0 was a little too high; the mean stayed near the 0.89 of the kernel before, and the first rival (VectorE over 1.21 us) is refuted. By the Trainium skill (GPSIMD Engine Reference, Key points) GpSimd contends with VectorE instructions that have two SBUF inputs. These rows agree: means of 0.68 to 1.50 us for such operations, and 0.685 for the row that reads PSUM. PE loses nothing by it here. The small waits of 5 us were too many: the whole stretch has 0.44.

**The writes.** They land in 2.8 us where 3.0 was taken, at 154 GB/s where 150 was, and ScalarE waits 11.8 us for them in all, about 1 us a pair. The threshold of 8 us, however, was too high: with three writes slots are held for 6.8 us in the median, and 66.7 us are lost. The margin is smaller than the prediction believed; how much of that loss is the fuller DMA's is open.

**The norm of the second half.** Predicted were 17 us of wait and 3 of clock. Between 1256 and 1300 us PE is idle for 44.00 - 28.52 = 15.5 us, and its 95 matmuls take 28.5 us instead of 95 x 0.2266 = 21.5, so 7.0 go to slower matmuls, most of them at the lower clock: 22.5 us. The clock's share was at the upper end of its range, the wait a little below. The weight sum ends at 1287.96, 33.6 us after the scale factor (1254.33), where about 31 were worked out. What ended the wait in the profile was the bank of m; the first experiment shows that the weight sum stands right behind it, and the third that with both gone the matmuls take nearly all of the time that the waits leave.

**The change of product.** Predicted were 6 us from an add behind the sides on VectorE. Measured were 4.8 of idle time and 1.6 of lower clock, 6.4, but the releaser was a load that SP issued late. The size was right for the wrong reason, which is luck; the run with earlier loads shows it. The prediction's own working there does not add up either: 2 x 0.69 + 11 x 0.7 is 9.1 and not 9.3, and the nine operations of its text are eleven in its sum.

**Out_proj.** Predicted were 2.5 us for a load and a split at the new pools, in a range to 6. It cost 5.9. The term was mis-sized because the weight's copy queued on ScalarE behind the copy of mh.

**The groups' changes** were costed at nothing. From 1700 to 1886 us PE is idle for 1.6 us in all, nearly all of it for a low part on GpSimd and none for a side.

**The tail** was put at 30 us for the half matmuls and what follows. From 1886.3 to the end it is 42.2 us, less 48 full matmuls (10.9): 31.3. The size is right, the reason in part. VectorE was to be the bound beside the half matmuls, but up to 1911.8 PE is never idle and VectorE is busy 18.28 of the 25.70 us. The excess comes behind the last matmul, 16.7 us where 10.8 were counted, and there VectorE's order decides (rows of the changed kernel, then one of the kernel before):

```profile
1904.85 5.35 DVE L1133 SCALAR_TENSOR_TENSOR o<-xa,vecs,ps 128x512 f32<-128x512 f32 x8
1910.13 1.41 DVE L1119 TENSOR_TENSOR xa<-ps,xa 128x256 f32<-128x256 f32 x4
...
1915.34 3.22 DVE L1133 SCALAR_TENSOR_TENSOR o<-xa,vecs,ps 128x256 f32<-128x256 f32 x8 [1.12 <-PE ps L214]
```

```profile
1945.07 3.22 DVE L947 SCALAR_TENSOR_TENSOR o<-xa,vecs,ps 128x256 f32<-128x256 f32 x8 [1.19 <-PE ps L154]
```

The first half's closing norm holds up the adds, and the norm of the quarter before last starts 3.5 us after the end of the last large matmul (1911.87); in the kernel before it started over 6 us ahead of it. Less work on VectorE is no cure by itself: the run with whole columns has less of it and takes 2.1 us longer.

By these steps the feed-forward part was to take 1908.5 - 1224.5 = 684.0 us, and it takes 687.3. The part ahead of it was to grow by 2.5 and grows by 5.9. Worked out from the stages alone the gain is 52.9 - 5.9 = 47 us, where the prediction had 53.7. The measured difference of the medians is 53.8. The rest is the start of the feed-forward part, which differs by more than that between profiles in which the work ahead of it is the same. So the mechanism and most of the terms are right, and that the median comes within 2 us of the forecast is in part luck.
